# A two-block transformer kernel: streams merged by a model of the engines in place of constants

## The chip, the cores and the metric

The kernel runs on one core of a Trainium2 chip. The metric is the device time of one execution in microseconds (us). Before the change it is 2180.11 us, the median of 3 runs (2177.14 to 2183.31).

## The reference

Two blocks follow each other on x of 512 tokens by 1024 features, all in fp32.

```python
# block 1
h = rms_norm(x, norm_pre)
(aq, ak, av, az, dq, dk, dv, db, da, dz, gate_att, gate_dn) = split_cols(h @ w_in)
q, k = rope(rms_norm(heads(aq))), rope(rms_norm(heads(ak)))          # 8 query, 2 key heads of 128
y_att = (softmax_attention(q, k, av) * silu(az)) @ w_br_att
cq, ck, cv = split(silu(short_conv(concat(dq, dk, dv), conv_w)))     # 5 taps
o_dn = chunked_gated_delta_rule(l2(cq), l2(ck), cv, g, beta)         # 8 heads, forward + backward
y_dn = (rms_norm(o_dn) * silu(dz)) @ w_br_dn
mix = (sigmoid(gate_att) * y_att + sigmoid(gate_dn) * y_dn) @ w_out
x = x + rms_norm(mix)
x = x + rms_norm(sigmoid(x @ w_ple_gate) * (p @ w_ple_proj))
# block 2: two layers; the mixer of the first is stick-breaking, of the second differential attention
for i in range(2):
    x = x + mixer[i](rms_norm(x))
    x = x + swiglu_ffn(rms_norm(x))                                  # width 2816
# stick-breaking, 16 heads of 64: z = q k^T * scale, earlier = key < query
#   weight = exp(log_sigmoid(z) + sum over later keys of log_sigmoid(-z)); out = weight @ v
# differential, 8 heads: a = softmax(q1 k1^T) - lam * softmax(q2 k2^T); out = rms_norm(a @ v)
```

## The kernel before

Activations lie with features on the 128 partitions and 512 tokens along a row. Each fp32 operand of a large product is split into a high and a low fp32r part, and a product is three matmuls (`mm3`). A weight tile of 128x1024 comes by a DMA of SP's queue (`wtile`), is cast by ScalarE to `whi`, and VectorE computes the rest `wlo`. These instructions are raised by 200 places in priority, so that they run ahead of the matmuls that need them.

Work is written as Python generators, called streams. One long stream per stage issues the projections, weight tile by weight tile. The others are short: a head's attention for one block of queries (`att_unit` in the first block, `unit` in the stick-breaking and the differential stage), transposes (`att_fm`, `to_fm`), and for the delta rule `dn_prep`, `dn_inv`, `dn_chain` and `dn_fin`. `Driver.run` merges them into one order. It holds a clock `t`, which `mm` and `transpose` advance by a duration for each matmul. A stream yields when it has to wait: a number is a delay from now; an `Event` is ready at the time that `set` gave it; a `Slots` object stands for PSUM banks (2 acc, 5 z, 1 o) or for chunks of SBUF, each free from the time that `release` or `drop` gave it. The driver resumes the stream with the earliest ready time; among equals the one that stands first in the list, and the projections stand last. No operation of VectorE, ScalarE or GpSimd advances the clock: what these take is in the constants of the yields, as `CH1 = CH2 = CH3 = 1.3` in `dn_chain`, `SB_LAT1 = 5.0` in the stick-breaking unit, `DF_LAT1 = 4.0`, `DF_LAT3 = 3.0`, `DF_LAT5 = 4.0` in the differential one, `ATT_LAT = 5.0` after an attention projection, 1.4 us before the matmuls of `dec`, 8.0 us around the inverse's transfers.

The merged order is the emission order, and the tile scheduler uses it as a priority: an instruction that its own account holds for ready may pass one that was emitted earlier.

A stick-breaking unit (L694 on) computes z on TensorE into a z bank, then on ScalarE and VectorE L714 to L717 and a split (L319, L320), then adds sums of the result to z with TensorE, takes exp (L733), and multiplies with v. `me["S"]` is the event that lets the next unit's first matmuls go, `me["PV"]` the one that keeps the products with v in order:

```python
            for i, c0 in its:
                head[i] = (sh[:, c0:c0 + T - P * i], sl[:, c0:c0 + T - P * i])
            drv.set(me["S"])
            yield SB_LAT1
```

In the differential unit (L1930 on), after the last block of queries of a head, the squares' sum goes to GpSimd for a power (L1839), VectorE scales the output to `os` (L2005), and `otr` transposes it.

Of the kernel before, what the change touches and what calls it, by code (L numbers as in the profile page):

```python
# [17 lines left out]
P = 128  # L18
# [28 lines left out]
CH1 = 1.3  # L47
# [49 lines left out]
class Driver:  # L97
# [2 lines left out]

    def __init__(self):
        self.t = 0.0

    def set(self, ev, lat=0.0):
        ev.t = self.t + lat

    def release(self, slots, lat=0.0, n=1):
        slots.free.extend([self.t + lat] * n)  # L110

    def spawn(self, g):

        self.tasks.insert(0, [g, self.t, None])

    def run(self, streams):
        tasks = self.tasks = [[g, 0.0, None] for g in streams]
        while tasks:
            best = None
            for k, (g, ready, need) in enumerate(tasks):  # L120
                if isinstance(need, Event):
                    if need.t is None:
                        continue
                    ready = max(ready, need.t)
                elif isinstance(need, Take):
                    if len(need.slots.free) < need.n:
                        continue
                    ready = max(ready, sorted(need.slots.free)[need.n - 1])
                key = (max(ready, self.t), k)
                if best is None or key < best[0]:  # L130
                    best = (key, k)
            if best is None:
                raise RuntimeError("streams wait for each other: " + str([(g.__name__, n) for g, _, n in tasks]))
            task = tasks[best[1]]
            self.t = max(self.t, best[0][0])
            g, _, need = task
            if isinstance(need, Take):
                need.slots.free.sort()
                del need.slots.free[:need.n]
            try:  # L140
                v = next(g)
            except StopIteration:
                tasks.remove(task)
                continue
            if isinstance(v, Slots):
                v = Take(v, 1)
            if isinstance(v, (Event, Take)):
                task[1:] = self.t, v
            else:
                task[1:] = self.t + (v or 0.0), None  # L150


class Raw:
# [14 lines left out]
class Net:  # L168
    def __init__(self, ctx, tc, ins, out):
        self.tc = tc  # L170
        self.nc = tc.nc
        self.ins = ins
        self.out = out
        self.drv = Driver()
        self.pre = None
        self.nw = 0

        self.wnext = []
        self.woff = WOFF
        self.w3 = None  # L180

        self.hold = None
        pool = lambda name, bufs, **k: ctx.enter_context(tc.tile_pool(name=name, bufs=bufs, **k))
        self.cp = pool("consts", 1)
        self.wst = pool("wst", WST)
        self.whi = pool("whi", WHI)
# [48 lines left out]

    def drop(self, n, lat=0.0):

        self.drv.release(self.mem, lat, n)

    def need(self, n):  # L240
        return Take(self.mem, n)
# [16 lines left out]
    def consts(self):  # L258
        nc = self.nc
        self.ident = self.cp.tile([P, P], F32, name="ident")  # L260
        make_identity(nc, self.ident)
# [24 lines left out]
        self.m_off = self.cp.tile([P, 32], F32, name="m_off")  # L286
        nc.vector.reduce_sum(self.m_off, mo.rearrange("p b j -> p j b"), axis=AX.X)
        self.m_ntri = self.cmask("m_ntri", ALU.is_ge, 1, 0, -1.0)
        self.negones = self.cp.tile([P, P], F32R, name="negones")
        nc.vector.tensor_scalar(out=self.negones, in0=self.ones, scalar1=-1.0, scalar2=None, op0=ALU.mult)  # L290


    def mm(self, out, lhsT, rhs, start, stop):
        n = 1
        for d in rhs.shape[1:]:
            n *= d
        if lhsT.dtype == F32R:
            self.drv.t += max(n * 0.42, 106 if lhsT.shape[-1] == P and lhsT.shape[0] == P else 54) / 1000
        else:
            self.drv.t += max(n * 1.67, 108) / 1000  # L300
        self.nc.tensor.matmul(out, lhsT=lhsT, rhs=rhs, start=start, stop=stop, skip_group_check=True)  # L301

    def transpose(self, out, in_):
        self.drv.t += 0.109
        self.nc.tensor.transpose(out, in_, self.ident)

    def mm3(self, out, ls, rs, start, stop):
# [14 lines left out]
    def wtile(self, ap, n=1024):  # L322

        nc = self.nc
        with self.tc.high_priority(offset=self.woff):
            st = self.wst.tile([P, 1024], F32, tag="st", name="st")
            nc.sync.dma_start(out=st[:, :n], in_=ap)
            self.nw += 1
            third = self.w3 is not None and self.nw % 4 == 0
            hi = (self.w3 if third else self.whi).tile([P, 1024], F32R, tag="hi", name="whi")  # L330
            lo = (self.w3 if third else self.wlo).tile([P, 1024], F32R, tag="lo", name="wlo")
            self.split(hi[:, :n], lo[:, :n], st[:, :n])
        return hi, lo

    def wtile_big(self, ap):
# [3 lines left out]
        with self.tc.high_priority(offset=WBOFF):  # L339
            for j in range(2):  # L340
                st = self.work("wbst")
                BQ(nc).dma_start(out=st, in_=ap[:, j * T:(j + 1) * T])
                hi, lo = self.chunk("wbhi", F32R), self.chunk("wblo", F32R)
                self.split(hi, lo, st)
                parts.append((hi, lo))
        return parts

# [785 lines left out]
    def dn_chain(self, S, hh, d):  # L1133
# [13 lines left out]
        for step in range(4):  # L1147
# [4 lines left out]
            if step:  # L1152
# [11 lines left out]
                                                   in1=ocol, op0=ALU.mult, op1=ALU.add)  # L1164
                R["seen"].add(n)
                drv.release(self.free["z"], CH1)
                yield CH1
            else:
                r = R["vt"][:, c]
            yield self.free["z"]  # L1170
# [4 lines left out]
            if step < 3:  # L1175
                vd = self.half("vd")
                nc.scalar.mul(vd, ps[:, 0:P], R["game"][:, d, n:n + 1])
            yield CH2
            if step < 3:
                self.mm(ps[:, P:2 * P], R["kt"][:, c], vd, True, True)  # L1180
            self.mm(ps[:, 2 * P:3 * P], R["a", d][:, c], vn, True, True)
# [11 lines left out]
                nc.vector.tensor_tensor(ocol, ps[:, 2 * P:3 * P], ocol, op=ALU.add)  # L1193
            R["seen"].add(n)
            drv.release(self.free["z"], CH3)
            yield CH3
        S["left", hh] -= 1
        if S["left", hh] == 0:
            self.drop(4 if S["b"] == 3 else 6, 1.0)
# [982 lines left out]
```

## Time and profile before

| what | value |
|---|---|
| median of 3 runs | 2180.11 us |
| the profiled execution | 2179.57 us, span 2177.9 us |
| TensorE busy | 2101.2 us, 96% |
| VectorE busy | 1231.3 us, 57% |
| ScalarE busy | 1000.5 us, 46% |
| GpSimd busy | 117.0 us, 5% |
| granted TensorE clock, mean | 0.987 |

The span runs from the first to the last instruction. The first block takes it to about 880 us (attention and delta rule to 620, branches and output to 820), the stick-breaking stage to 1170, its feed-forward to 1532, the differential stage to 1818, and the last feed-forward to the end. A matmul's busy time overlaps with that of the next one, since they are pipelined.

### The profile page before, as it was taken

The page shows a single profiled execution, that of the slowest core. Times are in us where ns is not written, and L with a number is a line of the kernel's source. Part 1 is how long each engine was busy: PE and PEld are TensorE (multiplying, and loading weights), DVE is VectorE, ACT ScalarE, POOL GpSimd, SP SyncE. Part 2 cuts the span into 40 slices and gives each one's busy share as a digit, 9 for nine tenths or more (in the row PEclk, how much of TensorE's full clock was granted, in tenths as well). Part 3 has the DMA queues.
Part 4 walks back from the last instruction along what each step waited for, and adds up shares of the span by engine and source line. Part 5 has one row for each costly group of instructions (what it writes and reads, how often), then busy time and mean ns, then how long its engine had stood idle before and what let it go on. Part 6 is the DMA issues. An engine that isn't in the chain of part 4 may idle for free.

```text
span 2177.9 us, 33391 instructions
## 1 busy us (share of the span) xinstructions
PE 2101.2 (96%) x13214; PEld 1804.9 (83%) x13214; DVE 1231.3 (57%) x2519; ACT 1000.5 (46%) x2015; POOL 117.0 (5%) x157
## 2 busy tenths in 40 slices
PE   7999999989999999899999999999999989999999
PEld 6798888879788877788878888888999878888887
DVE  8865865886542546855555444433577765444421
ACT  6556647555622355666664222222465643222211
POOL 2000110100000000000000000000111100000000
PEclk9999999999999999999999999999999999999999
DMA  4221121222334443011112222333211112333332
GB/s 154 73 81 50 46 75 50 62 78 62 103 105 142 148 153 107 14 46 59 53 45 97 97 95 95 91 95 99 88 59 51 52 54 97 97 97 96 92 110 71
DMA packets 73996, 181.72 MB, mean 83 GB/s; under 512 B 24176, under 2 KB 24816, under 8 KB 73840
## 3 DMA queue, kind: packets, MB, share of 16 engines
q1 hardware_dynamic: 72560, 175.40, 25.3%
q0 software_dynamic: 1280, 4.20, 0.6%
q8 instruction: 104, 1.70, 0.3%
q14 instruction: 52, 0.43, 0.1%
HBM read 170.13 MB, written 9.44 MB: 82 GB/s over the span
## 4 chain that ended last, share of the span: by engine, by line
PE 79%; DVE 11%; ACT 5%; issue 2%; POOL 2%; DMA 1%; SPq 0%; POOLq 0%; DVEq 0%; ACTq 0%
PE pg L301 17%; PE pd L301 11%; PE pu L301 11%; PE po L301 8%; PE pb L301 4%; PE z L301 3%; PE pv L301 3%; PE pz L301 3%; PE wS L301 2%; PE pk L301 2%; DVE wlo L320 2%; DVE cacc L845 2%; PE sb_q L301 2%; PE sb_k L301 1%; PE s L301 1%
## 5 line engine op out<-in xcount | busy, mean ns | idle before, releaser
L317 ACT CAST whi<-st 128x1024 fp32r<-128x1024 f32 (+1 forms) x295 | 305.8, 1039 | 796.1 <-issue 331.6
L320 DVE TENSOR_TENSOR wlo<-st,whi 128x1024 fp32r<-128x1024 f32 (+1 forms) x295 | 356.3, 1209 | 279.7 <-ACT whi L317 275.6
L301 PE MATMUL pg<-rlo,whi 128*128 128x512 f32 x352 | 138.7, 394 | 0.0
L301 PE MATMUL pg<-rhi,whi 128*128 128x512 f32 x352 | 138.1, 392 | 0.0
L301 PE MATMUL pg<-rhi,wlo 128*128 128x512 f32 x352 | 137.9, 392 | 0.0
L301 PE MATMUL pd<-mh,wlo 128*128 128x512 f32 x352 | 137.5, 391 | 0.0
L301 PE MATMUL pd<-mh,whi 128*128 128x512 f32 x352 | 137.5, 391 | 0.0
L301 PE MATMUL pd<-ml,whi 128*128 128x512 f32 x352 | 137.5, 391 | 0.0
L301 PE MATMUL pu<-rhi,wlo 128*128 128x512 f32 x352 | 137.2, 390 | 0.0
L301 PE MATMUL pu<-rlo,whi 128*128 128x512 f32 x352 | 137.1, 389 | 0.0
L301 PE MATMUL pu<-rhi,whi 128*128 128x512 f32 x352 | 137.0, 389 | 0.0
L2050 DVE TENSOR_TENSOR sg<-pg,rfm 128x512 f32<-128x512 f32 x44 | 30.4, 692 | 118.2 <-PE pg L301 118.1
L2056 DVE TENSOR_TENSOR m<-pu,sg 128x512 f32<-128x512 f32 x44 | 30.4, 692 | 115.4 <-PE pu L301 115.4
L301 PE MATMUL pv<-whi,rhi 128*128 128x256 f32 x256 | 75.9, 297 | 3.3 <-ACT tmq L1868 2.1
L301 PEld LDWEIGHTS pg<-rhi,wlo 128*128 128x128 f32 x352 | 66.2, 188 | 15.1 <-issue 0.5
L301 PEld LDWEIGHTS pg<-rlo,whi 128*128 128x128 f32 x352 | 66.3, 188 | 15.0 <-issue 0.5
L301 PEld LDWEIGHTS pg<-rhi,whi 128*128 128x128 f32 x352 | 66.2, 188 | 14.5
L301 PEld LDWEIGHTS pd<-ml,whi 128*128 128x128 f32 x352 | 66.2, 188 | 14.3
L301 PEld LDWEIGHTS pd<-mh,wlo 128*128 128x128 f32 x352 | 66.1, 188 | 14.3
L301 PEld LDWEIGHTS pd<-mh,whi 128*128 128x128 f32 x352 | 66.1, 188 | 14.2
L301 PEld LDWEIGHTS pu<-rhi,whi 128*128 128x128 f32 x352 | 66.1, 188 | 14.0
L301 PEld LDWEIGHTS pu<-rlo,whi 128*128 128x128 f32 x352 | 66.1, 188 | 14.0
(563 smaller groups left out, 5820.8 us busy)
## 6 DMA issues: line engine op xcount, KB each, us to landing
st<-w_gate SPq DMA_DIRECT2D x44, 512.0 KB, 3.4
st<-w_up SPq DMA_DIRECT2D x44, 512.0 KB, 3.5
st<-w_down SPq DMA_DIRECT2D x32, 512.0 KB, 3.6
st<-w_dn SPq DMA_DIRECT2D x24, 512.0 KB, 3.6
st<-w_out SPq DMA_DIRECT2D x24, 512.0 KB, 3.5
st<-w_down SPq DMA_DIRECT2D x16, 384.0 KB, 3.1
x<-xT SPq DMA_DIRECT2D x16, 256.0 KB, 6.5
st<-w_aq SPq DMA_DIRECT2D x8, 512.0 KB, 3.6
```

The source lines that it names most:

```text
L301: self.nc.tensor.matmul(out, lhsT=lhsT, rhs=rhs, start=start, stop=stop, skip_group_check=True)
L317: nc.scalar.copy(hi, src)
L320: nc.vector.tensor_tensor(lo, src, hi.bitcast(F32), op=ALU.subtract)
L845: nc.vector.scalar_tensor_tensor(out=acc[:, a], in0=raw[:, b], scalar=w[:, s:s + 1], in1=acc[:, a], op0=ALU.mult, op1=ALU.add)
L2050: nc.vector.tensor_tensor(sg, ps, self.rfm, op=ALU.mult)
L2056: nc.vector.tensor_tensor(m, ps, sg, op=ALU.mult)
```

## The change

The driver gets a model of the three other engines. Every vector, scalar, gpsimd and sync instruction that the kernel issues passes through a wrapper (`Modelled`), which calls `Driver.op` with its output and inputs. `op` takes the latest modelled end of the inputs, places a duration worked out from the width into the first hole of that engine's list of busy times, and keeps the end under the output's name. What a step issued then sets its events, its delays and its releases: where a step issued such an instruction, a number that it yields is replaced by the modelled end of the step's work, and so is the delay in `set` and `release` (a PSUM bank is free from the end of the last operation that reads PSUM). A stream can also yield a tile and is ready when that tile is. The split of a weight tile is marked as early: its ready time lies 4 us before now, and it doesn't count as the step's work. The durations of matmuls change too. No instruction's operands or engines change.

```diff
 class Driver:
+        self.done = {}
+        self.busy = {e: [] for e in ("vector", "scalar", "gpsimd")}
+    def place(self, engine, ready, cost):
+        b = self.busy[engine]
+        while b and b[0][1] < self.t - 20:
+            b.pop(0)
+        at = ready
+        for k, (x, y) in enumerate(b):
+            if at + cost <= x:
+                b.insert(k, (at, at + cost))
+                return at
+            at = max(at, y)
+        b.append((at, at + cost))
+        return at
+    def op(self, engine, fn, out, ins):
+        ready = self.t - 4.0 if self.early else self.t
+        for a in ins + ([out] if fn == "accumulate" else []):
+            ready = max(ready, self.done.get(a.tensor.name, 0.0))
+        width = lambda a: math.prod(a.shape[1:])
+        if fn == "dma_start":
+            end = ready + 2.2
...
+            if engine == "vector":
+                cost, more = 0.065 + n / 960, 0.09
+                if fn in ("tensor_scalar", "scalar_tensor_tensor"):
+                    cost += 0.055
+            elif engine == "scalar":
+                cost, more = 0.1 + n / 1220, 0.1
+            else:
+                cost, more = (0.3 + 0.17 * n if fn == "tensor_tensor" else 0.1 + n / 500), 0.05
+            end = self.place(engine, ready, cost) + cost + more
+        self.done[out.tensor.name] = max(end, self.done.get(out.tensor.name, 0.0))
+        if not self.early and self.task is not None:
+            self.task.end = max(self.task.end, end)
+            self.task.has = True
+            if any(a.space == PSUM for a in ins):
+                self.task.bank_end = max(self.task.bank_end, end)
     def set(self, ev, lat=0.0):
-        ev.t = self.t + lat
-    def release(self, slots, lat=0.0, n=1):
-        slots.free.extend([self.t + lat] * n)
+        ev.t = max(self.t, self.task.end) if self.task is not None and self.task.has else self.t + lat
+    def release(self, slots, lat=0.0, n=1, bank=True):
+        t = self.t + lat
+        if self.task is not None and self.task.has:
+            t = max(self.t, self.task.bank_end if bank else self.task.end)
+        slots.free.extend([t] * n)
     def run(self, streams):
...
+            task.need, task.ready = None, self.t
             if isinstance(v, (Event, Take)):
-                task[1:] = self.t, v
+                task.need = v
+            elif v is None or isinstance(v, (int, float)):
+                if v:
+                    task.ready = max(self.t, task.end) if task.has else self.t + v
             else:
-                task[1:] = self.t + (v or 0.0), None
+                for a in v if isinstance(v, tuple) else (v,):
+                    task.ready = max(task.ready, self.done.get(a.tensor.name, 0.0))
...
     def mm(self, out, lhsT, rhs, start, stop):
         if lhsT.dtype == F32R:
-            self.drv.t += max(n * 0.42, 106 if lhsT.shape[-1] == P and lhsT.shape[0] == P else 54) / 1000
+            self.drv.t += max(n / 2400 + 0.013, 0.06)
+        elif lhsT.shape[0] == 32:
+            self.drv.t += 0.033
         else:
-            self.drv.t += max(n * 1.67, 108) / 1000
+            self.drv.t += max(n * 0.00167, 0.11)
+        self.drv.done[out.tensor.name] = self.drv.t + 0.2
...
     def wtile(self, ap, n=1024):
+            self.drv.early = True
             self.split(hi[:, :n], lo[:, :n], st[:, :n])
+            self.drv.early = False
...
     def dn_chain(self, S, hh, d):
-                yield CH1
+                yield r
...
-            yield CH2
+            yield (vn, vd) if step < 3 else vn
...
-            yield CH3
+            yield st if step < 3 else CH3
```

## Rows read from the trace of the kernel before

**Rows 1.** The page: busy us (share) and count; chain that ended last.

```profile
PE 2101.2 (96%) x13214; PEld 1804.9 (83%) x13214; DVE 1231.3 (57%) x2519; ACT 1000.5 (46%) x2015; POOL 117.0 (5%) x157
...
PE 79%; DVE 11%; ACT 5%; issue 2%; POOL 2%; DMA 1%; SPq 0%; POOLq 0%; DVEq 0%; ACTq 0%
```

**Rows 2.** Windows: stretch, length, busy us (x) PE, PEld, DVE, ACT, POOL, clock, DMA.

```profile
60.00:430.00 370.00, 355.58 (x3261) 319.84 (x3260) 262.27 (x637) 221.42 (x623) 27.48 (x22) 1.00 0.20 60
430.00:620.00 190.00, 177.03 (x1913) 156.24 (x1912) 126.61 (x367) 107.63 (x298) 9.30 (x10) 0.95 0.27 82
...
940.00:1136.00 196.00, 194.88 (x1106) 166.22 (x1104) 106.09 (x176) 121.48 (x226) 7.46 (x18) 1.00 0.15 49
1170.00:1532.00 362.00, 362.00 (x1585) 297.32 (x1584) 155.39 (x183) 104.26 (x131) 0.00 (x0) 1.00 0.31 95
1532.00:1775.00 243.00, 224.90 (x1732) 214.65 (x1730) 177.97 (x598) 139.94 (x284) 43.76 (x41) 0.98 0.18 57
```

**Rows 3.** Windows: the same columns, 4 us of the differential stage.

```profile
1666.00:1670.00 4.00, 4.00 (x24) 4.00 (x23) 2.47 (x16) 1.56 (x3) 3.12 (x4) 0.58 0.00 0
```

**Rows 4.** Timeline: start, us, engine, line, operation, [idle before <-releaser].

```profile
1662.33 1.01 POOL L1839 TENSOR_TENSOR f<-f,mhalf 128x4 f32<-128x4 f32 x1
...
1664.05 0.68 DVE L2005 TENSOR_TENSOR os<-po,f 128x512 f32<-128x512 f32 x1
...
1664.79 0.66 PE L305 MATMUL otr<-ident,os 128*128 128x128 f32 x4 [2.10 <-DVE os L2005]
```

**Rows 5.** Timeline of ScalarE in the stick-breaking stage.

```profile
1031.01 0.59 ACT L714 ACTIVATE t<-z 128x512 f32<-128x512 f32 x1
1031.49 0.52 ACT L716 ACTIVATE t<-t 128x384 f32<-128x384 f32 x1
```

**Rows 6.** Chain of waits in time order: start, us, what; the feed-forward stage.

```profile
1181.53 5.44 PE pg L301 x24
```

**Rows 7.** Waits of TensorE, 60 to 620: us in total, times, longest.

```profile
PE dec L301 <- DVE gm L913: 3.7, 3, 1.4
PE tr L305 <- DVE tmq L1311: 3.4, 2, 2.6
PE tr L305 <- DVE s L1215: 2.8, 2, 1.5
...
PE tp L305 <- ACT e L1364: 1.4, 4, 0.7
PE Q L301 <- ACT aux L1089: 1.3, 2, 1.1
```

**Rows 8.** Tiles r and wS: duration ns min/median/max, first and last start us.

```profile
L1158 DVE SCALAR_TENSOR_TENSOR r<-kS,neg_eg,vt x48: 329/342/352, 206.6 to 600.4; 128x128 f32<-128x128 f32 x48
...
L1174 ACT ACTIVATE vn<-wS,gam x64: 358/368/464, 201.9 to 602.5; 128x128 f32<-128x128 f32 x64
```

**Rows 9.** Waits of TensorE, 1532 to 1775.

```profile
PE otr L305 <- DVE os L2005: 10.7, 5, 2.5
PE tp L305 <- DVE e L1963: 2.8, 2, 1.9
```

**Rows 10.** Tile t, 940 to 1136: duration ns min/median/max.

```profile
L714 ACT ACTIVATE t<-z x38: 473/492/598, 941.3 to 1124.6; 128x384 f32<-128x384 f32 x25, 128x512 f32<-128x512 f32 x13
L715 ACT ACTIVATE t<-t x38: 513/531/632, 941.8 to 1125.2; 128x384 f32<-128x384 f32 x25, 128x512 f32<-128x512 f32 x13
L716 ACT ACTIVATE t<-t x38: 512/536/640, 942.7 to 1125.9; 128x384 f32<-128x384 f32 x25, 128x512 f32<-128x512 f32 x13
L717 DVE SCALAR_TENSOR_TENSOR t<-z,t x38: 548/557/692, 943.3 to 1126.5; 128x384 f32<-128x384 f32 x25, 128x512 f32<-128x512 f32 x13
L319 DVE CAST sh<-t x38: 351/360/428, 943.9 to 1127.3; 128x384 fp32r<-128x384 f32 x25, 128x512 fp32r<-128x512 f32 x13
L320 DVE TENSOR_TENSOR sl<-t,sh x38: 545/559/693, 944.3 to 1127.7; 128x384 fp32r<-128x384 f32 x25, 128x512 fp32r<-128x512 f32 x13
```

**Rows 11.** Window 940 to 1136, tile z alone: length, PE, PEld, DVE, ACT.

```profile
940.00:1136.00 196.00, 64.02 (x404) 55.23 (x404) 22.73 (x38) 39.23 (x76) 1.00 0.15 49
```

More of the change, by code (lines that the diff above doesn't have):

```diff
@@ L104, in __init__ @@
         self.t = 0.0
-    def set(self, ev, lat=0.0):
-        ev.t = self.t + lat
-    def release(self, slots, lat=0.0, n=1):
-        slots.free.extend([self.t + lat] * n)
+        self.done = {}
+        self.busy = {e: [] for e in ("vector", "scalar", "gpsimd")}
+        self.end = self.bank_end = 0.0
+        self.early = False
+        self.task = None
+    def place(self, engine, ready, cost):
[10 more added lines that the diff above has]
+        return at
@@ new lines, in op @@
+    def op(self, engine, fn, out, ins):
[5 more added lines that the diff above has]
+            end = ready + 2.2
+            if engine == "gpsimd":
+                self.place(engine, ready, 0.55)
+        else:
+            n = max([width(out)] + ([width(ins[0])] if fn in ("tensor_reduce", "reduce_sum") else []))
+            if engine == "vector":
[4 more added lines that the diff above has]
+                cost, more = 0.1 + n / 1220, 0.1
+            else:
+                cost, more = (0.3 + 0.17 * n if fn == "tensor_tensor" else 0.1 + n / 500), 0.05
[6 more added lines that the diff above has]
+                self.task.bank_end = max(self.task.bank_end, end)
@@ L112, in spawn @@
+    def set(self, ev, lat=0.0):
+        ev.t = max(self.t, self.task.end) if self.task is not None and self.task.has else self.t + lat
[4 more added lines that the diff above has]
+        slots.free.extend([t] * n)
     def spawn(self, g):
-        self.tasks.insert(0, [g, self.t, None])
+        self.tasks.insert(0, Task(g, self.t))
@@ L116, in run @@
     def run(self, streams):
-        tasks = self.tasks = [[g, 0.0, None] for g in streams]
+        tasks = self.tasks = [Task(g, 0.0) for g in streams]
         while tasks:
             best = None
-            for k, (g, ready, need) in enumerate(tasks):
+            for k, task in enumerate(tasks):
+                need, ready = task.need, task.ready
                 if isinstance(need, Event):
@@ L130, in run @@
                 if best is None or key < best[0]:
-                    best = (key, k)
+                    best = (key, task)
             if best is None:
-                raise RuntimeError("streams wait for each other: " + str([(g.__name__, n) for g, _, n in tasks]))
-            task = tasks[best[1]]
+                raise RuntimeError("streams wait for each other: " + str([(t.g.__name__, t.need) for t in tasks]))
+            task = self.task = best[1]
             self.t = max(self.t, best[0][0])
-            g, _, need = task
+            need = task.need
             if isinstance(need, Take):
@@ L139, in run @@
                 del need.slots.free[:need.n]
+            task.has = False
             try:
-                v = next(g)
+                v = next(task.g)
             except StopIteration:
@@ L144, in run, with __init__, __getattr__, issue @@
                 continue
+            finally:
+                self.task = None
             if isinstance(v, Slots):
                 v = Take(v, 1)
+            task.need, task.ready = None, self.t
             if isinstance(v, (Event, Take)):
-                task[1:] = self.t, v
-            else:
-                task[1:] = self.t + (v or 0.0), None
+                task.need = v
+            elif v is None or isinstance(v, (int, float)):
+                if v:
+                    task.ready = max(self.t, task.end) if task.has else self.t + v
+            else:
+                for a in v if isinstance(v, tuple) else (v,):
+                    task.ready = max(task.ready, self.done.get(a.tensor.name, 0.0))
+class Task:
+    def __init__(self, g, ready):
+        self.g, self.ready, self.need = g, ready, None
+        self.end = self.bank_end = 0.0
+        self.has = False
+class Modelled:
+    def __init__(self, engine, name, drv):
+        self._engine, self._name, self._drv = engine, name, drv
+    def __getattr__(self, fn):
+        real = getattr(self._engine, fn)
+        if not callable(real):
+            return real
+        def issue(*args, **kw):
+            res = real(*args, **kw)
+            aps = [a for a in args if hasattr(a, "tensor")]
+            out = kw["out"] if "out" in kw else aps.pop(0) if aps else None
+            if out is not None:
+                ins = aps + [v for k, v in kw.items() if k not in ("out", "accum_out") and hasattr(v, "tensor")]
+                self._drv.op(self._name, fn, out, ins)
+                if "accum_out" in kw:
+                    self._drv.done[kw["accum_out"].tensor.name] = self._drv.done[out.tensor.name]
+            return res
+        return issue
+class Engines:
+    def __init__(self, nc, drv):
+        self.real = nc
+        self.tensor = nc.tensor
+        for name in ("vector", "scalar", "gpsimd", "sync"):
+            setattr(self, name, Modelled(getattr(nc, name), name, drv))
 class Raw:
@@ L170, in __init__ @@
         self.tc = tc
-        self.nc = tc.nc
+        self.drv = Driver()
+        self.nc = Engines(tc.nc, self.drv)
         self.ins = ins
         self.out = out
-        self.drv = Driver()
         self.pre = None
@@ L236, in drop @@
     def drop(self, n, lat=0.0):
-        self.drv.release(self.mem, lat, n)
+        self.drv.release(self.mem, lat, n, False)
     def need(self, n):
@@ L260, in consts @@
         self.ident = self.cp.tile([P, P], F32, name="ident")
-        make_identity(nc, self.ident)
+        make_identity(nc.real, self.ident)
         self.neg30 = self.cp.tile([P, P], F32R, name="neg30")
@@ L297, in mm @@
         if lhsT.dtype == F32R:
-            self.drv.t += max(n * 0.42, 106 if lhsT.shape[-1] == P and lhsT.shape[0] == P else 54) / 1000
-        else:
-            self.drv.t += max(n * 1.67, 108) / 1000
+            self.drv.t += max(n / 2400 + 0.013, 0.06)
+        elif lhsT.shape[0] == 32:
+            self.drv.t += 0.033
+        else:
+            self.drv.t += max(n * 0.00167, 0.11)
+        self.drv.done[out.tensor.name] = self.drv.t + 0.2
         self.nc.tensor.matmul(out, lhsT=lhsT, rhs=rhs, start=start, stop=stop, skip_group_check=True)
     def transpose(self, out, in_):
-        self.drv.t += 0.109
+        self.drv.t += 0.11
+        self.drv.done[out.tensor.name] = self.drv.t + 0.2
         self.nc.tensor.transpose(out, in_, self.ident)
@@ L343, in wtile_big @@
                 hi, lo = self.chunk("wbhi", F32R), self.chunk("wblo", F32R)
+                self.drv.early = True
                 self.split(hi, lo, st)
+                self.drv.early = False
                 parts.append((hi, lo))
```

## The prediction

> **What bounds the kernel now.** I read the page's first part and the chain of waits, then the busy time by stage, then who TensorE waits for, and last the tiles of two stages. The page shows TensorE busy for 96% of the span and carrying 79% of the chain that ended last [rows 1]. So any other engine counts only through TensorE's stops. The table by stage says where these are [rows 2]. The feed-forward stage (1170 to 1532 us) has none: one stream, nothing to merge. Idle TensorE (stretch less busy time) is 14.4 us in 60 to 430 and 13.0 us in 430 to 620 (attention and delta rule of the first block), 1.1 us in 940 to 1136 (stick-breaking), 18.1 us in 1532 to 1775 (differential attention). That is 45.5 us in three merged stretches, 2.1% of the span, and about all a better merge can win, with what the clock gives: the granted clock is 0.95 in 430 to 620 and 0.98 in 1532 to 1775 [rows 2]. In one such place it was 0.58 for 4 us [rows 3], near the lower of its two levels (1.2 of 2.4 GHz), right behind a stop of 2.1 us [rows 4].
>
> **The change part by part.** No computing instruction is added or removed. What changes is the order in which the streams emit, because the merge's clock and the ready times differ. Emission order is a priority, not a law: in the stick stage ScalarE follows L714 of a 512-wide unit with L716 of a 384-wide one [rows 5], while a unit emits 714, 715, 716 together. So a ready time that is too late costs little, and TensorE stops mainly where something is thought ready that isn't.
>
> *The clock.* A 512-wide fp32r matmul was counted as 0.42 ns a column, 0.215 us; now it is 0.226. The feed-forward row has 24 in 5.44 us, 0.227 each [rows 6]. So the old clock ran 5% fast beside projections, and every constant was in truth 5% longer; the new one is right. That alone moves no instruction by more than some tenths of a us: I cost it at nothing. The Trainium skill (TensorE: Matmul & The Clock Gate, Back-to-back issue gap) speaks against this edit: it gives an isolated gap of N/2.4 + 2.5 ns, 215.8 ns for 512, which is the old constant. By that rule the new clock would be 5% slow and plan streams in early; by the row it is right, the measurement decides, and the sum has nothing from it either way.
>
> *First block, ready times by operand.* The stops named in 60 to 620 that come from a stream put in before its operand was there are the masks of dec 3.7, the transposes of tmq 3.4 and of the value tile 2.8, the attention weights 1.4, Q 1.3: 12.6 us [rows 7]. Each followed a constant (1.4, 5.0, 5.5, 2.5 us) that ignored how busy VectorE was. The model places these operations into VectorE's modelled time, so such streams come later and a projection goes ahead. Not all can go: the model fits an operation into the first hole, whereas an engine runs its queue in order behind weight splits (the ready time of an early split is t − 4, but its tile's own transfer is booked at t + 2.2 outside that mark, so splits are booked later than they run). And ATT_LAT stays a constant, since its step issues nothing. I take two thirds, −8.4 us; ends: nothing, and all idle of the two stretches, −27.4.
>
> *The chain's hops.* In dn_chain 1.3 us becomes the operand's modelled end. The parts are short: 0.34 us for r, 0.37 for vn [rows 8], so a hop falls to about 0.6 to 0.8 us. No wait for these stands among TensorE's longest in that stretch [rows 7]: nothing to win, and the cover is the 1.3 us itself. There are 48 r, 64 vn and 32 later states, 144 hops; 0.1 us short in each is +14. Earlier chains could close the stops in 430 to 620, already counted. Since a matmul that isn't ready can be passed, I take 0, nearest to the missing rows; ends 0 and +14.
>
> *Differential attention.* TensorE waits 10.7 us in five places for the scaled output os and 2.8 for the probabilities [rows 9]. In the stop shown GpSimd finishes f at 63.3, behind the power of another tile, os follows at 64.05 and otr at 64.79 after 2.1 us of idle [rows 4]. The model carries both powers at 0.3 + 0.17 a column (0.98 us for 4, against 1.01 in the row). But a late otr needs other matmuls to go ahead: with projections still left it has them, in the last head it hasn't. I take two stops like the shown one with their 0.2 us of refilled pipeline, −4.6; ends −13.5, and, since the constants 3.0 and 4.0 shrink to the modelled ends, a 2.1 us stop in all eight heads: 16.8 − 10.7 = +6.1.
>
> *Granted clock.* Lost are 0.05 × 190 = 9.5 us and 0.02 × 243 = 4.9 us [rows 2], 14.4 in all. With a good third of the stops gone I take a third, −4.8; ends −14.4 and 0.
>
> *Stick-breaking, the part that speaks against the change.* The line that sets me["S"] stands behind the unit's elementwise operations. Before, it gave the merge's own time, so the next unit's first matmuls could be emitted at once and up to five units share the five z banks. Now it gives the modelled end of the whole sequence, so units become serial in the plan: Abs, Exp, Ln, max-add, cast, difference have medians 0.49 + 0.53 + 0.54 + 0.56 + 0.36 + 0.56 = 3.04 us [rows 10], and TensorE's own z work is 64.0/38 = 1.68 us a unit [rows 11]. 4.7 us against the pace of 196/38 = 5.16 us a unit: only 0.4 us is left for queueing, with ScalarE 62% and VectorE 54% busy [rows 2]. One wait of 0.25 us before each of the six operations makes 6.2 us, and the 48 units would fall 48 × 1.04 = 50 us behind the projections. That is the upper end. But late units still overlap among themselves, as a later unit's ready matmuls pass, and their TensorE work is the same 2 us or so; what remains is a tail with little to fill its stops. I take +6 us, near the rows of a stage that has only 1.1 us of idle; ends −1.1 and +50.
>
> Sum: −8.4 + 0 − 4.6 − 4.8 + 6 = −11.8. From the profiled execution's 2179.57 this is 2167.8; its time lies 0.5 below the median of the runs (2180.11), so I say 2168. The span (2177.9) has 1.7 us around it that stay.
>
> **The rivals.**
> *Slower, by the serial units.* Mechanism as above: the units of the stick stage end behind the projections, and the output projection, which needs all of them, starts later than 1136 us. It decides from a unit's modelled round above 5.16 us. For it: the 0.4 us of room. Against it: the passing of blocked matmuls. Half of the 50 us, less 7 us of the gains: 2180 + 25 − 7 = 2198.
> *No change.* TensorE's order is mostly set by one long projection stream, and what the old constants left is in places where nothing else is ready: the tail of each stage, the reduction ahead of each norm. Then the gains and the 6 us cancel, about 2179, within 6.5 us.
> *A larger gain.* The modelled times fit nearly everywhere: two thirds of the 45.5 us idle and of the 14.4 us of clock, −40 us: 2140. For it: five wait rows alone carry 12.6 us [rows 7]. Against it: weight splits, loads and tails are among the stops and don't depend on the merge.
> *It doesn't do what it says.* Where a step issues nothing on the three engines the old constant stays, so part of the plan is unchanged. That leads to the case of no change, and is counted there.
>
> **How the numbers follow.** Forecast 2168: 0.38, own range 2155 to 2174. Larger gain 0.12, no change 0.20, slower 0.30. A difference of 0.3%, 6.5 us, is about what a measurement of this kernel can tell from none. Faster: 0.38 + 0.12 = 0.50; same 0.20; slower 0.30. The range reaches from below the larger gain to above the slower case, 2134 to 2204; outside are the full win of every stop and the unmitigated lag of 50 us, one in ten each.
>
> **What would show it.** Right: the waits for gm, tmq and os shrink to less than half of their rows; idle in 430 to 620 falls below 9 us and its clock rises to 0.97 or more. In the stick stage, ScalarE runs the three functions of one unit without another's between them. Wrong: that stage ends more than 10 us later against its start; waits of TensorE for r, vn or S appear with several us; the clock in 940 to 1136 leaves 1.00. The prediction as a whole fails if the stick stage loses more than the first block and the differential stage win.

## The result and the profile after

The changed kernel takes 2249.38 us (median of 4 runs, 2246.21 to 2250.19) against 2181.71 for the kernel before (4 runs, three of them those of the 2180.11 above): 1.0311 times its time [1.0291, 1.0331]. Forecast was 2168, range 2134 to 2204. So the sign is wrong and the time lies outside the range, beyond the rival that had this sign (2198).

The page of the kernel after (busy us, share and count; then the chain that ended last), against [rows 1]:

```profile
PE 2140.5 (95%) x13214; PEld 1820.5 (81%) x13214; DVE 1243.2 (55%) x2519; ACT 1015.0 (45%) x2015; POOL 119.0 (5%) x157
...
PE 75%; DVE 12%; ACT 7%; issue 3%; POOL 3%; DMA 1%; SPq 0%; POOLq 0%; DVEq 0%; ACTq 0%
```

The counts are the same, so only order and waiting changed; ScalarE's share of the chain rose from 5% to 7%, TensorE's fell from 79% to 75%. Where the 69.5 us of span went is read from the starts of each stage's first matmuls in both traces:

| stage, us | before | after | difference |
|---|---|---|---|
| first block, to its last branch product | 757.6 | 765.6 | +8.0 |
| end of the first block, to the first product of the stick-breaking stage | 118.5 | 117.0 | −1.5 |
| stick-breaking | 293.3 | 350.5 | **+57.2** |
| its feed-forward | 362.7 | 362.7 | 0 |
| differential | 279.1 | 285.0 | +5.9 |
| last feed-forward | 362.5 | 362.5 | 0 |

A stage differs a little from one trace to the next even where its instructions are the same: the first block of e2 below, whose code is that of the kernel before, takes 754.8 us in its one trace, 2.8 less than 757.6. Differences of 3 us or less are therefore not read.

The table by stage of the kernel after (columns as in [rows 2]; from the stick-breaking stage on stretches are moved by the delay; 1076 to 1196 is new):

```profile
60.00:430.00 370.00, 356.73 (x3272) 321.21 (x3271) 264.75 (x641) 225.60 (x622) 26.00 (x22) 1.00 0.20 62
430.00:620.00 190.00, 173.21 (x1859) 151.16 (x1858) 123.66 (x359) 104.77 (x297) 9.94 (x10) 0.90 0.25 75
...
940.00:1136.00 196.00, 184.57 (x977) 150.88 (x976) 100.29 (x159) 115.54 (x203) 7.60 (x18) 0.97 0.15 49
...
946.00:1076.00 130.00, 130.00 (x732) 111.51 (x730) 72.41 (x111) 81.93 (x139) 6.56 (x16) 1.00 0.19 62
1076.00:1196.00 120.00, 96.17 (x372) 65.08 (x371) 44.35 (x82) 55.21 (x107) 0.00 (x0) 0.81 0.02 5
...
1596.00:1839.00 243.00, 222.83 (x1726) 212.50 (x1724) 179.89 (x594) 140.55 (x283) 45.52 (x40) 0.99 0.17 56
```

Read two things. 430 to 620 did not gain: 16.8 us idle for 13.0, clock 0.90 for 0.95 [rows 2]. And the stick-breaking stage falls in two: from 946 to 1076 us TensorE has no gap at all, then come 120 us in which no engine is busy throughout (TensorE 96, ScalarE 55, VectorE 44 us), the clock is 0.81 and hardly a weight moves (5 GB/s). That is the tail that the prediction spoke of: the projections are through, units are left. The kernel before has the same 120 us of its own span full:

```profile
1076.00:1196.00 120.00, 118.56 (x554) 95.86 (x554) 68.99 (x101) 63.03 (x102) 0.00 (x0) 1.00 0.22 71
```

The tile of the exp that each of the 48 units ends its elementwise work with, before (first row) and after, here up to the end of the last key projection and behind it (name, count, ns min/median/max, first and last start):

```profile
L733 ACT ACTIVATE w<-z x48: 469/493/606, 921.0 to 1131.3; 128x384 f32<-128x384 f32 x32, 128x512 f32<-128x512 f32 x16
```

```profile
L236 ACT ACTIVATE w<-z x23: 467/492/598, 928.4 to 1072.6; 128x384 f32<-128x384 f32 x16, 128x512 f32<-128x512 f32 x7
...
L236 ACT ACTIVATE w<-z x25: 491/492/601, 1079.3 to 1193.2; 128x384 f32<-128x384 f32 x16, 128x512 f32<-128x512 f32 x9
```

(After, all elementwise instructions carry line 236, the wrapper's.) Before, a unit ended every (1131.3 − 921.0)/47 = 4.47 us. After, beside projections, every (1072.6 − 928.4)/22 = 6.55 us, so that 25 of 48 are left when the projections end; then every (1193.2 − 1079.3)/24 = 4.75 us. The mean, 264.8/47 = 5.63 us, is 1.16 us more, and 48 × 1.16 = 56 us is the stage's loss.

What fills one such round (the time from one unit to the next, here 4.6 us) is on the timeline of that tail (start, us, engine, line, what, [idle before <-releaser]):

```profile
1119.81 0.60 ACT L236 ACTIVATE w<-z 128x512 f32<-128x512 f32 x1 [2.58 <-PE z L408]
1120.30 0.48 ACT L236 ACTIVATE t<-z 128x384 f32<-128x384 f32 x1
...
1120.82 1.08 ACT L236 ACTIVATE t<-t 128x384 f32<-128x384 f32 x2
...
1121.02 0.74 PE L408 MATMUL z<-qs,kh 128*128 128x384 f32 x1
...
1121.78 0.22 PE L408 MATMUL z<-m_ge,neg 128*128 128x128 f32 x1
1121.93 0.56 DVE L236 SCALAR_TENSOR_TENSOR t<-z,t 128x384 f32<-128x384 f32 x1 [2.72 <-ACT t L236]
...
1122.94 0.33 PE L408 MATMUL z<-sh,negones 128*128 128x128 f32 x1 [0.94 <-DVE sh L236]
...
1124.42 0.49 ACT L236 ACTIVATE w<-z 128x384 f32<-128x384 f32 x1 [2.53 <-PE z L408]
1124.81 0.48 ACT L236 ACTIVATE t<-z 128x384 f32<-128x384 f32 x1
```

One unit runs from 1120.30 (its Abs) to its exp at 1124.42: ScalarE, VectorE, TensorE, ScalarE, one after the other. The next unit's z is complete at 1122.00, and ScalarE has nothing to do from 1121.90; yet its Abs waits until 1124.81, behind the exp that it stands behind in ScalarE's queue. TensorE did pass the blocked sums, a unit ahead; ScalarE passed nothing, so it idles 2.5 to 3.6 us in each of the rounds from 1119 to 1135 us. The trace has this order in all 48 units: ScalarE runs Abs, Exp, Ln and the last exp of one unit with no other unit's between them, whereas before up to five units' last exps stand in a row. TensorE's waits of 900 to 1233 us show the same ring from its side; of these three (first fence) the kernel before, from 900 to 1170 us, has one, z for `t`, once, with 0.2 us (second):

```profile
PE po L408 <- ACT w L236: 10.6, 17, 0.7
PE z L408 <- DVE t L236: 7.6, 10, 1.6
PE z L408 <- DVE sh L236: 3.7, 5, 0.9
```

```profile
PE z L301 <- DVE t L717: 0.2, 1, 0.2
```

### The profile page after: what moved, and what is told of

It reads as the page before. It is cut to its first block, busy times and chain, and to the rows that moved or that the text cites. A ratio compares the mean times of both kernels' runs of the same rounds, so it can differ in the third digit from the quotient of the medians.

```text
span 2247.4 us, 33322 instructions
## 1 busy us (share of the span) xinstructions
PE 2140.5 (95%) x13214; PEld 1820.5 (81%) x13214; DVE 1243.2 (55%) x2519; ACT 1015.0 (45%) x2015; POOL 119.0 (5%) x157
## 4 chain that ended last, share of the span: by engine, by line
PE 75%; DVE 12%; ACT 7%; issue 3%; POOL 3%; DMA 1%; SPq 0%; POOLq 0%; DVEq 0%; ACTq 0%
PE pg L408 17%; PE pd L408 11%; PE pu L408 11%; PE po L408 8%; PE pb L408 4%; PE z L408 3%; PE pv L408 2%; PE pz L408 2%; PE sb_q L408 2%; DVE cacc L236 2%; PE wS L408 2%; DVE wlo L236 2%; PE sb_k L408 2%; ACT t L236 1%; ACT whi L236 1%
## 5 line engine op out<-in xcount | busy, mean ns | idle before, releaser
L236 DVE SCALAR_TENSOR_TENSOR t<-z,t 128x384 f32<-128x384 f32 (+1 forms) x48 | 28.9, 602 | 118.5 <-ACT t L236 118.4
```

Of the source, the lines that this page charges most:

```text
L236: res = real(*args, **kw)
```

## The experiments

Theory 1 was that the late event of the stick-breaking units is nearly all of the loss. Undone alone in the kernel after, and put alone into the kernel before:

```diff
 # e1, from the kernel after               # e2, from the kernel before
-            drv.set(me["S"])
+            me["S"].t = drv.t
-            drv.set(me["S"])
+            drv.set(me["S"], SB_LAT1)
```

> The changed kernel with one line altered: in the stick-breaking unit me["S"] gets the merge's own time again, so the next unit's first matmuls may be emitted at once; all else keeps the model. Theory 1 (the units became serial in the plan by this event): the stage from the first sb_q to the first gate matmul of the feed-forward falls from 322 us back to 262 to 272, ScalarE works on several units in bursts again, and the time is about 2249 - 57 = 2192 (2185 to 2200). Rival (modelled bank releases and the modelled waits within a unit spread the units, the event does not matter): the stage stays above 300 us and the time above 2230.

> The kernel before with one line altered: in the stick-breaking unit me["S"] is set 5.0 us later (SB_LAT1) instead of now; constants, no model. Theory 1: this alone brings the loss, some 6 to 7 us from unit to unit while projections last, about 25 units left when they end, and 2181 + 45 to 65 = 2226 to 2246. Rival (the model does it, not the event): within 10 us of the kernel before.

Measured: e1 2195.86 us, 1.0065 [1.0049, 1.0081] of before, 53.5 less than after. e2 2239.78 (one run, so no interval), 58.6 more than before. The stretch 1076 to 1196 in e1, then in e2, and e2's longest waits of TensorE in 900 to 1225:

```profile
1076.00:1196.00 120.00, 118.69 (x571) 96.80 (x570) 69.67 (x102) 66.91 (x109) 1.04 (x2) 1.00 0.22 71
```

```profile
1076.00:1196.00 120.00, 90.01 (x330) 60.09 (x331) 40.80 (x76) 51.98 (x99) 0.00 (x0) 0.79 0.00 1
```

```profile
PE po L301 <- ACT w L733: 13.0, 21, 0.7
PE z L301 <- DVE t L717: 12.4, 16, 1.6
```

With the event at once the same stretch is full and its clock 1.00: projections last to 1118 us, and 6 of the 48 units are left then. With constants everywhere and a late event the tail and the waits appear, and all 48 units stand one behind the other on ScalarE, as in after (7.3 us from unit to unit beside projections, 28 left behind them; 6 to 7 us and about 25 were expected). In e1 ScalarE mixes units again (Abs, Exp, then the next unit's Abs, 0.95 us after the first):

```profile
1097.95 0.49 ACT L236 ACTIVATE t<-z 128x384 f32<-128x384 f32 x1 [0.70 <-PE z L408]
1098.47 0.52 ACT L236 ACTIVATE t<-t 128x384 f32<-128x384 f32 x1
1098.90 0.47 ACT L236 ACTIVATE t<-z 128x384 f32<-128x384 f32 x1
```

So theory 1 held, from both sides. What remained was e1's 0.65%, in the traces 7.0 us of the first block and 6.6 of the differential stage.

**The matmul durations, alone.** e3 puts all new durations into the kernel before, e8 only those of fp32r:

```diff
-            self.drv.t += max(n * 0.42, 106 if ... else 54) / 1000
+            self.drv.t += max(n / 2400 + 0.013, 0.06)          # e3 and e8
+        elif lhsT.shape[0] == 32:
+            self.drv.t += 0.033                                 # e3
```

> The kernel before with only the durations of matmuls and transposes changed as in the change (n/2400 + 0.013 for fp32r, 0.033 for 32 rows, 0.11 at least for fp32); constants stay. The prediction costed this at nothing: 2176 to 2187. Rival (the faster or slower clock shifts every constant, and the first block's 7 us come from it): the first block ends at least 5 us later, time 2187 or more.

> The kernel before with only the fp32r durations of the change; 32-row and other fp32 matmuls stay at 0.108 us. It splits the 23 us that the whole clock cost. If the loss is the fp32r part (projections counted 5 to 11% longer, so constants become relatively shorter and streams come in earlier): 2200 to 2207. If it is the 32-row part (the inverse counted 15 us shorter a batch): within 5 us of 2181.

Measured: 2204.54, 1.0115 [1.0092, 1.0137], and 2200.92, 1.0088 [1.0071, 1.0105]. The edit that I had costed at nothing costs 23 us when the constants stay, 19 of them by fp32r alone. In e3 the first block has 11.5 us of it (769.1 against 757.6), the differential stage 7.8, the stick-breaking stage 4.5.

**The other events.** e4 takes e1 and sets the event at once in the units of the first block and of the differential stage too (`me["S"].t = drv.t` in all three):

> The changed kernel with me["S"] at the merge's own time in all three kinds of units (stick-breaking, softmax attention of the first block, differential). Theory 1 extended (the same event also costs the first block its 6.4 us and the differential stage its 5.8): 2249 - 57 - 12 = 2180. Theory 1 for the stick stage alone (in the other two there is filling work enough, their losses have other causes): the same as with the stick event alone, about 2192.

Measured: 2181.35, 1.0003 [0.9993, 1.0013]. The differential stage fell from 285.7 us in e1 to 272.0, 7.1 below before; the first block kept its loss (764.6 us in e1, 764.3 in e4). So in the differential stage the event hid a gain.

**What the first block loses.** e5 gives the inverse of the delta rule its constants back (the two delays of 8.0 us around transfers, and the row loop's), e6 those of `dn_chain`, e7 the old durations of matmuls, each from e4. A `Fixed` number is a delay from now, as before the change:

```diff
-                    task.ready = max(self.t, task.end) if task.has else self.t + v
+                    task.ready = max(self.t, task.end) if task.has and not isinstance(v, Fixed) else self.t + v
...
-        yield 8.0                                        # e5, e9
+        yield Fixed(8.0)
-            yield INV_SLOW * (0.4 + i * i * 0.00208)     # e5, e10
+            yield Fixed(INV_SLOW * (0.4 + i * i * 0.00208))
-        yield INV_LAT                                    # e5, e9
+        yield Fixed(INV_LAT)
-                yield r                                  # e6, with CH2 and CH3
+                yield Fixed(CH1)
```

> All events at the merge's time, and in dn_inv the three delays around the transfers and the row loop (8.0, the loop's, INV_LAT 8.0) stay constants instead of modelled ends. Theory 2 (the rest of the first block's loss, 757.6 to 764.3 us at the last branch matmul, is the inverse put in too early, since the model books a transfer at 2.2 us and no time of SP's queue): the 6.5 us wait of M for xt goes, the first block ends at 755 to 759, time 2173 to 2177. Rival (the chain's short hops, which keep TensorE on small matmuls with stops and the clock low): first block unchanged within 2 us, time 2179 to 2184.

> All events at the merge's time, and dn_chain yields its constants of 1.3 us again in place of the operands r, vn, vd and the state. Theory 2: unchanged within 3 us of 2181, the wait of M for xt stays. Rival (the hops): the stretch at the lower clock behind 565 us goes, first block ends 4 to 7 us earlier, time 2174 to 2178.

> All events at the merge's time, with the model of the engines, but the matmul durations of the kernel before. Theory 3 (the constants of before had been chosen with the old clock, and only with constants does the new clock cost; the model supplies waits in true time, so it wants the true clock): slower than 2181 by 5 us or more. Rival (the durations as such merge worse, with or without the model): faster than 2176.

Measured: e5 2162.5, 0.9911 [0.9896, 0.9926]; e6 2182.97, 1.0004 [0.9993, 1.0014]; e7 2182.87, 1.0004 [0.9994, 1.0014]. e5 gained more than its expectation allowed (first block 745.8 us). The hops count for nothing that can be told, and with the model in place the durations don't either, in the total: both expectations on e7 missed. (By stage, e7's differential one is 5.1 us longer than e4's, 277.1 against 272.0.) The inverse is the place, and e9 (its transfers alone) and e10 (its row loop alone) split it:

> All events at the merge's time, and in dn_inv only the two delays that cover transfers (8.0 ahead of the row loop and INV_LAT 8.0 behind it) stay constants; the row loop's delays are modelled. Theory 2a (the transfers: the model has 2.2 us for each and nothing for SP's queue): most of the 18.5 us that the three constants brought, first block ends at 745 to 751, time 2162 to 2168. Rival 2b (the row loop, 7 us modelled against 15 in constants): first block stays above 757, time above 2174.

> All events at the merge's time, and in dn_inv only the row loop's delays stay constants. Theory 2a: little of the gain, first block above 757, time above 2174. Rival 2b: first block at 745 to 751, time 2162 to 2168. If both runs come to about 2171, the inverse just has to come later by some 8 us, whatever it is that delays it.

Measured: e9 2179.97, 1.0 [0.9989, 1.001]; **e10 2161.01 (2156.68 to 2163.38), 0.9903 [0.9886, 0.9921]**, with e5, whose runs overlap with its own, the fastest of all and faster than both kernels. It is the loop's ready times: 30 VectorE instructions that each need the one before, followed by transfers, a transpose to `xt` and the matmuls of `M`. The model gives it 2 × (15 × 0.155 + 1240/960) = 7.2 us where VectorE's modelled time is free, the constants 1.7 × (15 × 0.4 + 1240 × 0.00208) = 14.6. In the trace of after, the third of four such loops (its first and last instructions, the one ahead of its longest gap, then what follows):

```profile
443.05 0.15 DVE L236 TENSOR_TENSOR Lt<-L 128x1 f32<-128x1 f32 x1
...
481.08 0.35 DVE L236 TENSOR_REDUCE L<-Lt 128x14 f32<-128x196 f32 x1
...
490.51 0.54 DVE L236 TENSOR_TENSOR Lt<-L 128x225 f32<-128x225 f32 x1
...
493.12 0.38 DVE L236 TENSOR_REDUCE L<-Lt 128x15 f32<-128x225 f32 x1
...
509.27 0.70 DVE L236 STREAM_TRANSPOSE xt<-xd 128x512 f32<-128x512 f32 x1
...
510.03 1.93 PE L408 MATMUL M<-xt,ud 32*32 32x32 f32 x128 [6.67 <-DVE xt L236]
```

It takes 493.50 − 443.05 = 50.5 us, its instructions 0.15 to 0.54 us each: the rest is nearly all its turn among VectorE's other work (VectorE is busy for 45.6 of these 50.5 us, with 83 other instructions). TensorE then waits 6.67 us, its longest wait of the stage. In e10 the same loop takes 25.0 us:

```profile
434.95 0.15 DVE L240 TENSOR_TENSOR Lt<-L 128x1 f32<-128x1 f32 x1
...
459.51 0.40 DVE L240 TENSOR_REDUCE L<-Lt 128x15 f32<-128x225 f32 x1
...
470.87 0.70 DVE L240 STREAM_TRANSPOSE xt<-xd 128x512 f32<-128x512 f32 x1
```

The stretch 430 to 620 of e4, then of e10:

```profile
430.00:620.00 190.00, 173.50 (x1861) 151.40 (x1860) 123.83 (x357) 103.41 (x295) 9.92 (x10) 0.90 0.25 73
...
430.00:620.00 190.00, 180.14 (x1936) 157.57 (x1935) 122.73 (x358) 106.79 (x297) 9.53 (x10) 0.96 0.28 85
```

No wait for `xt` is left among e10's, the stretch has 9.9 us of idle for e4's 16.5 and a clock of 0.96 for 0.90: 6.6 us of idle and, as an estimate, 0.06 × 190 = 11 us of clock, most of the 20 us that the first block is shorter by than in e4. It takes 744.2 us, 13.4 below before. That last difference isn't the loop's length: in the kernel before the third loop took 24.1 us, about as in e10.

**Is it the length of the constants?** e12 is e8 with every constant of the driver times 1.08 (about what the clock was lengthened by), e13 the kernel before with the same factor and its old durations, e14 e8 with the loop's factor `INV_SLOW` at 1.84 in place of 1.7:

```diff
-        ev.t = self.t + lat                              # e12, e13
+        ev.t = self.t + lat * 1.08
-                task[1:] = self.t + (v or 0.0), None
+                task[1:] = self.t + (v or 0.0) * 1.08, None
-INV_SLOW = 1.7                                           # e14
+INV_SLOW = 1.84
```

> The kernel before with the change's fp32r durations (which cost 18 us) and every constant (delays, events, releases) 8% longer, which is about what the projections' durations grew by (5% at 512 columns, 11% at 256). Theory 3 (the clock as such costs nothing; the constants became relatively too short): back to within 6 us of 2182. Rival (any other plan than the one that the constants were chosen for loses some 20 us): 2195 or more.

> The kernel before, its clock kept, every constant 8% longer. It tells the gain of longer constants from that of the truer clock. If it is the constants' length that wins, whichever the clock: 2160 to 2170. If clock and constants have to fit each other (theory 3): within 6 us of 2182 or slower. If the merge answers to any small shift with some 20 us of either sign: 2195 or more is as likely.

> The kernel before with the change's fp32r durations and only the row loop's constant 8% longer (INV_SLOW 1.84 in place of 1.7). If the row loop is the place where the clock's 18 us are lost, as it was with the model: 2164 to 2180. If not: 2195 to 2206.

Measured: e12 2163.73, 0.9919 [0.9903, 0.9935]; e13 2169.38, 0.9954 [0.9937, 0.997]; e14 2188.64, 1.0038 [1.0023, 1.0053]. Both expectations on e12 missed, e14 fell between its two, e13 met its first. Against e8's 2200.92 the loop's factor alone gives 12 us back, all constants 37. So constants longer by 8% win with either clock, and the new durations beside the old constants, which shorten these in proportion, lose. That the old constants were too short fits this. It isn't shown for more than this one length: a merge that answers any small shift with some 20 us of either sign, the third expectation of e13, is less likely, since all three lengthenings won, but it was not tried by other lengths. That the durations are better as such is not shown: e12 is ahead of e13, but e7 finds no difference.

**A queue more in the model.** e11 places each DMA of e4 for 0.45 us into a modelled SP queue:

```diff
+            if engine == "sync":
+                ready = self.place(engine, ready, 0.45) + 0.45
```

> All events at the merge's time, every delay modelled, and the model gets SP's queue: 0.45 us a transfer, in the first hole, then 2.2 us to landing. The eight reads of a step then end 3.6 us later in the plan. Theory 2a: a part of the gain, time 2165 to 2176. Rival (the transfers' real delay is waiting behind weight loads in the queue, which the model does not see): 2178 to 2184.

Measured: 2189.86, 1.0039 [1.0024, 1.0053], slower than without (e4, 2181.35). Both expectations missed; why it is slower was not looked for.

## Why the prediction was wrong, step by step

- *Stick-breaking: +6 forecast, +57.2 measured. This is the step that failed.* Its round was right (4.7 us without queueing, 4.6 to 4.75 in the tail; 6.2 with it, 6.55 beside projections), and its upper end of 50 came near, in part by luck: the pace of 196/38 = 5.16 us that it is measured against is too long. The 38 units of [rows 10] start from 941.3 to 1124.6, which is 4.95 us a unit, and over all 48 it is 4.47, so even a round of 4.7 left no room; against that, 6.55 us held for 23 of the 48 units and not for all. What was wrong is the sentence that cut it to 6, "late units still overlap among themselves, as a later unit's ready matmuls pass". Passing was looked at on TensorE alone. The ring goes through ScalarE, and there the next unit's Abs ran behind this one's exp. By the code, the event now has the very time at which the unit itself resumes, and among equals the earlier unit goes first, so its exp is emitted ahead of the next unit's Abs. The row that I took for free passing (L714 of one unit ahead of L716 of another [rows 5]) showed instructions emitted under an event at once; it was no evidence for a late one.
- *The rival* named this mechanism and its deciding point (a round above 5.16 us; 6.55 came), and halved the price for the same wrong reason. At the full price it said 2180 + 50 − 7 = 2223, still 26 below what came, since the gains of 7 didn't come either.
- *Clock: 0 forecast.* Wrong beside constants (e3, +23 us), right in the total inside the change (e7). The argument that no instruction moves by more than some tenths of a us looked at one constant; a stream is a chain of them, as the 15 of the row loop, and in e14 0.14 on that loop's factor, 1.2 us over the loop, is worth 12 us.
- *First block: −8.4 forecast, +8.0 measured.* The five named waits fell from 12.6 us [rows 7] to 4.4, by the 8.2 or so that were forecast (`gm` from 3.7 to 0.5, `tmq` from 3.4 to 1.1). What was wrong is the silent step from these rows to the block's time: other waits came in their place, so idle in the two stretches did not fall (27.4 us before, 30.1 after), and the clock's fall from 0.95 to 0.90 in 430 to 620 is, as an estimate, 0.05 × 190 = 9.5 us. What is late next was not asked:

```profile
PE M L408 <- DVE xt L236: 6.7, 1, 6.7
PE tr L413 <- DVE dk L236: 5.1, 3, 1.9
...
PE tr L413 <- DVE tmq L236: 1.1, 3, 0.5
...
PE wS L408 <- DVE r L236: 1.0, 1, 1.0
...
PE dec L408 <- DVE gm L236: 0.5, 1, 0.5
```

  The loop is the same kind of step as the one that was weighed: a chain whose model fits each operation into a hole and has no queue in order. With its constants back the block gains 13.4 us, within the end of 27.4 (e10).
- *Hops: 0 forecast, none that can be told measured* (e6 2182.97 against e4's 2181.35). One wait of 1.0 us for `r` appeared and cost nothing that can be told.
- *Granted clock: −4.8 forecast.* It fell to 0.90 in 430 to 620, and to 0.81 in a stretch that had stood at 1.00. In e10 it rises to 0.96.
- *Differential: −4.6 forecast, +5.9 measured,* made of about +13 from the late event (e1 against e4) and −7.1 from the rest of the change; with the old durations this rest is −2.0 (e7), too little to tell from none. I had asked about that event in one stage only. TensorE's waits for `os` fell from 10.7 [rows 9] to 6.3 us ahead of `otr` and 2.1 ahead of `po`, others grew (1596 to 1845 us of after):

```profile
PE otr L413 <- DVE os L236: 6.3, 2, 3.9
PE tp L413 <- DVE e L236: 3.6, 4, 2.6
PE po L408 <- ACT at L236: 3.0, 5, 2.0
...
PE po L408 <- DVE os L236: 2.1, 1, 2.1
```

- *The signs to look for.* Of those for it, the waits for `gm` and `tmq` fell to less than half; the wait for `os` did not halve, and in 430 to 620 the idle time rose and the clock fell. One unit's three functions did run without another's between them, but that was the wrong sign to choose: it is the serial order itself, which cost 57 us. Of those against it, two came, a stage over 10 us longer and a clock of 0.97 in 940 to 1136; the waits for `r`, `vn` or S, with several us, did not (one, 1.0 us). In the stick-breaking stage other waits came, for `w`, `t` and `sh`. The stick-breaking stage lost 57.2 us while the first block and the differential stage won nothing, by which the prediction was to fail as a whole.

What stays open: why the third loop meets 50 us of turns in VectorE's queue in after and 25 in e10 is seen only as far as the order goes; which emitted instruction sets it was not tried. It goes with the loop's delays in every trace of this case: 43.6 to 50.5 us in the seven where they are modelled (after, e1, e4, e6, e7, e9, e11), 22.7 to 25.5 in the nine where they are constants. Where the first block's gain beyond the kernel before comes from in e10 is open too. Nor was the model mended (a loop priced with its queue); e10 only puts numbers back.

## What to carry to other kernels

When a line of a scheduler changes from "now" to "when this is done", write down the ring that it closes, engine by engine, and its period against the pace of the stream beside it: here ScalarE's order made the whole ring serial, although TensorE passed blocked sums in it. A model in place of constants must carry what the constants paid for: the loop's constants came to 14.6 us and its four batches in the kernel before took 12.0 to 24.1, while the model gave it 7.2. If a discount on a worked-out price rests on one row, ask whether that row was recorded under the condition that the change takes away.

## What the runs showed of the hardware

A chain of 30 dependent VectorE instructions, 8 us of work by their own durations, took 10.0 to 50.5 us in the four batches of one execution (after), with gaps of up to 9.1 us between two of them while VectorE was busy with others. And the clock in the tail of after is not the mean 0.81 of its row but one level or the other (1116 to 1126, 1128 to 1135; columns as in [rows 2]):

```profile
1116.00:1126.00 10.00, 6.47 (x32) 4.54 (x31) 3.29 (x6) 4.74 (x10) 0.00 (x0) 0.99 0.00 0
...
1128.00:1135.00 7.00, 6.18 (x20) 4.34 (x18) 1.81 (x3) 2.44 (x5) 0.00 (x0) 0.50 0.01 2
```

It stood at the upper level (2.4 GHz) through rounds with 3.5 us of idle in 10, and a few us later at the lower one (1.2 GHz). The same kind of matmul and weight load in the two (weight loads of 128x128 take 0.19 us at the upper level there, mostly 0.33 at the lower):

```profile
1124.05 0.22 PE L408 MATMUL z<-sh,m_ntri 128*128 128x128 f32 x1
1124.06 0.19 PEld L408 LDWEIGHTS z<-sl,m_ntri 128*128 128x128 f32 x1
...
1132.32 0.41 PE L408 MATMUL z<-sl,negones 128*128 128x128 f32 x1
1132.42 0.33 PEld L408 LDWEIGHTS z<-sh,negones 128*128 128x128 f32 x1
```

What TensorE did before it fell is in the waits above: rounds with mean stops of 0.6 us for `w` and 0.7 to 0.8 us for `t` and `sh`. With these gone (e1), all 120 us are granted 1.00.
